# Sliding windows of a 2D image: loading the input in bands of 8 rows, issued between the stores

## The chip, the cores and the metric

One core of one Trainium2 chip runs the kernel. The metric is device time in microseconds (us) of one execution, as the median of several runs. The profile comes from one profiled execution; times in it count from the first instruction.

## The reference

The input `x` is float32 of shape (16, 64, 64, 64): image, channel, row, column. With a window of 8 and a stride of 4 there are 15 x 15 window positions, and each window is copied out:

```python
for i in range(n_h):
    for j in range(n_w):
        h_start = i * stride
        w_start = j * stride
        result[:, i, j] = x[:, :, h_start:h_start + window_size, w_start:w_start + window_size].copy()
```

Nothing is computed. 16.78 MB are read and 58.98 MB written, since each inner value stands in four windows.

## The kernel before, in words

The 128 partitions are 16 images x 8 channel groups; each partition holds 8 channels (`CLO`) of one image. The tile `L` has the whole input, 8 x 64 x 64 floats or 128 KB a partition, in one buffer that is written once.

Two DMAs fill it (lines 41 and 42), both issued on SP's queue: the upper 32 rows of every channel, then the lower 32. In memory 32 rows of a channel lie together, so a DMA consists of 128 x 8 runs of 8 KB.

Then 225 windows follow, row `i` outside and column `j` inside (lines 46 and 47). For each one VectorE copies the 8 x 8 x 8 floats of a window from `L` into a tile `g` (line 50), and a DMA stores `g` (line 51). In the output the 512 floats of a partition lie together, so a store is 128 runs of 2 KB, 256 KB in all. The pool of `g` has 28 buffers; a copy waits until the store of its buffer's last use has landed. Stores are issued in turn by SP (even windows) and ScalarE (odd ones): each of the two has a queue of its own, in the profile q1 (SP) and q10 (ScalarE; its sequencer is called ACTq).

What sets the order: each engine runs its own list of instructions in order, and the framework makes these lists when it builds the program, with a plan of its own of when each instruction could start. It follows the program text where an instruction can start by that plan, and takes a later one of the same engine first where it can't. So the order on a queue needn't be that of the text. In the built program SP's first store stands behind many of ScalarE's stores, and the last 20 stores of the list are all SP's.

The program has eight semaphores for these DMAs and gives them out in turn, in the planned order, over both queues. Before a DMA is issued, its queue waits until the DMA eight places earlier in that order has landed, whichever queue that was on. So at most eight are in flight. A copy waits for just those loads that wrote the part of `L` that it reads: the windows that lie in the upper 32 rows wait for the first load alone.

On the queue of an issuing engine everything waits behind the instruction at its head.

Of the kernel before, what the change touches and what calls it, by code (L numbers as in the profile page):

```python
# [1 line left out]

# [4 lines left out]


@with_exitstack  # L10
def kernel(
    ctx: ExitStack,
    tc: tile.TileContext,
    x: bass.AP,
    window_size: int,
    stride: int,
    out: bass.AP,
):
    nc = tc.nc
    P = nc.NUM_PARTITIONS  # L20

    B, C, H, W = x.shape
    Bo, NH, NW, Co, WSo, WSo2 = out.shape
    WS = int(window_size)
    ST = int(stride)
    assert Bo == B and Co == C and WSo == WS and WSo2 == WS

    f32 = mybir.dt.float32

    CHI = P // B  # L30
    CLO = C // CHI
    assert CHI * B == P and CLO * CHI == C

    lpool = ctx.enter_context(tc.tile_pool(name="lpool", bufs=1))
    gpool = ctx.enter_context(tc.tile_pool(name="gpool", bufs=28))

    L = lpool.tile([P, CLO, H, W], f32)

    HHALF = H // 2
    x_v = x.rearrange("b (ch cl) h w -> b ch cl h w", ch=CHI)  # L40
    nc.sync.dma_start(out=L[:, :, 0:HHALF, :], in_=x_v[:, :, :, 0:HHALF, :])
    nc.sync.dma_start(out=L[:, :, HHALF:H, :], in_=x_v[:, :, :, HHALF:H, :])

    trig = [nc.sync, nc.scalar]
    k = 0
    for i in range(NH):
        for j in range(NW):
            g = gpool.tile([P, CLO, WS, WS], f32, name="g")
            src = L[:, :, i * ST : i * ST + WS, j * ST : j * ST + WS]
            nc.vector.tensor_copy(out=g[:, :, :, :], in_=src)  # L50
            trig[k % 2].dma_start(out=out[:, i, j, :, :, :], in_=g[:, :, :, :])  # L51
            k += 1


# [1 line left out]
_INS = ['x', 'window_size', 'stride']  # L56
_OUTS = [((16, 15, 15, 64, 8, 8), 'float32')]
#: Inputs that are plain numbers.
_NUMBERS = {'window_size': 8, 'stride': 4}


# [26 lines left out]
```

## Time and profile before

| what | us |
|---|---|
| median of 3 runs | 221.94 (220.55, 221.94, 222.03) |
| span of the profiled execution, first to last instruction | 217.7 |
| VectorE busy | 88.7 |

The page of the profile gives the span of the profiled execution and no total of its own; the runs' median is 4.2 us above the span. A DMA packet in the profile is one run of bytes that one of the 16 DMA engines moves; the completion of a DMA is a small packet of its own on each engine. "Share" of a queue is the time of its packets over the time of 16 engines, so the shares of two queues can add to more than 100% where packets overlap.

### The profile page before, as it was taken

Reading aid. Unit: us, or ns where it says so; the run is one execution under the profiler, and the core shown is the slowest. Engines: PE = TensorE matmul, PEld = TensorE weight load, DVE = VectorE, ACT = ScalarE, POOL = GpSimd, SP = SyncE. Lnnn points to the kernel's source line nnn. Section 1 sums busy time; section 2 is a strip of 40 time slices with the busy share of each in tenths; the row PEclk is TensorE's granted clock in tenths of the full one; section 3 lists DMA queues with packets and bytes.
Section 4 is the critical chain, followed back from the end, with each engine's and each line's share of the span. In section 5 each row is a group of like instructions: output and inputs, shape, how many; then the busy total and the mean of one; then the engine's idle time right before and its main releaser. Section 6 shows DMA issues by size and latency. Waiting matters only on the chain.

```text
span 217.7 us, 824 instructions
## 1 busy us (share of the span) xinstructions
DVE 88.7 (41%) x225; POOL 0.2 (0%) x4
## 2 busy tenths in 40 slices
DVE  0000691124532446454565555555554554550000
POOL 0000000000000000000000000000000000000000
DMA  6999999989995999999999999999999999999997
GB/s 200 431 425 422 422 423 429 416 311 318 339 345 166 287 321 356 349 353 361 353 358 362 364 354 354 358 355 365 345 341 334 363 363 347 349 343 337 329 338 252
DMA packets 34487, 75.83 MB, mean 348 GB/s; under 512 B 3632, under 2 KB 3632, under 8 KB 32432
## 3 DMA queue, kind: packets, MB, share of 16 engines
q1 hardware_dynamic: 18352, 46.41, 59.0%
q10 hardware_dynamic: 16128, 29.37, 39.2%
q14 instruction: 7, 0.06, 0.1%
HBM read 16.78 MB, written 58.98 MB: 348 GB/s over the span
## 4 chain that ended last, share of the span: by engine, by line
DMA 82%; DVE 7%; issue 1%; DVEq 0%; ACTq 0%
DMA out_dram<-g 72%; DMA L<-in_x_dram 10%; DVE g L50 7%; DVEq L50 0%; ACTq L51 0%
## 5 line engine op out<-in xcount | busy, mean ns | idle before, releaser
L50 DVE COPY g<-L 128x512 f32<-128x512 f32 x225 | 88.7, 424 | 108.0 <-DMA out_dram<-g 83.4
L69 POOL MEMSET const-bfloat16-1.0<- 128x1 bf16 x1 | 0.1, 102 | 0.0
L69 POOL MEMSET const-uint8-127<- 128x1 uint8 x1 | 0.1, 102 | 0.0
L69 POOL MEMSET const-float32-1.0<- 128x1 f32 x1 | 0.1, 99 | 0.0
L69 POOL MEMSET const-float32-0.0<- 128x1 f32 x1 | 0.1, 98 | 0.2 <-issue 0.2
## 6 DMA issues: line engine op xcount, KB each, us to landing
out_dram<-g SPq DMA_DIRECT2D x113, 256.0 KB, 5.5
out_dram<-g ACTq DMA_DIRECT2D x112, 256.0 KB, 5.2
L<-in_x_dram SPq DMA_DIRECT2D x2, 8192.0 KB, 33.9
```

The source lines that it names most:

```text
L50: nc.vector.tensor_copy(out=g[:, :, :, :], in_=src)
L69: nc = _bacc.Bacc("TRN2", target_bir_lowering=False, num_devices=1)
```

## The change

The input is loaded in eight bands of 8 rows, each in four DMAs of two channels (512 KB, 256 runs of 2 KB), which go to SP and ScalarE in turn. The first band is issued ahead of everything. Every other band is issued in four pieces among the windows of the band before it: ahead of windows 0, 3, 6 and 9 of 15 for the first band, ahead of windows 0, 7, 14 and 21 of 30 for the later ones. The windows are taken in the same order as before; a band `n` brings window rows 2n - 1 and 2n. The pool of `g` has 36 buffers in place of 28.

```diff
@@ -29,33 +29,45 @@
 
     CHI = P // B
     CLO = C // CHI
-    assert CHI * B == P and CLO * CHI == C
+    RB = 8
+    NB = H // RB
+    assert CHI * B == P and RB == 2 * ST and WS == RB
 
     lpool = ctx.enter_context(tc.tile_pool(name="lpool", bufs=1))
-    gpool = ctx.enter_context(tc.tile_pool(name="gpool", bufs=28))
+    gpool = ctx.enter_context(tc.tile_pool(name="gpool", bufs=36))
 
     L = lpool.tile([P, CLO, H, W], f32)
+    x_v = x.rearrange("b (ch cl) (n r) w -> n (b ch) cl (r w)", ch=CHI, n=NB)
+    queues = [nc.sync, nc.scalar]
+    NP = 4
+    cw = CLO // NP
 
-    HHALF = H // 2
-    x_v = x.rearrange("b (ch cl) h w -> b ch cl h w", ch=CHI)
-    nc.sync.dma_start(out=L[:, :, 0:HHALF, :], in_=x_v[:, :, :, 0:HHALF, :])
-    nc.sync.dma_start(out=L[:, :, HHALF:H, :], in_=x_v[:, :, :, HHALF:H, :])
+    def load(n, k):
+        cs = slice(k * cw, (k + 1) * cw)
+        queues[k % 2].dma_start(out=L[:, cs, n * RB : (n + 1) * RB, :], in_=x_v[n, :, cs, :])
 
-    trig = [nc.sync, nc.scalar]
-    k = 0
-    for i in range(NH):
-        for j in range(NW):
+    for k in range(NP):
+        load(0, k)
+
+    t = 0
+    for n in range(NB):
+        rows = [i for i in (2 * n - 1, 2 * n) if 0 <= i < NH]
+        windows = [(i, j) for i in rows for j in range(NW)]
+        every = len(windows) // NP
+        for m, (i, j) in enumerate(windows):
+            if n + 1 < NB and m % every == 0 and m // every < NP:
+                load(n + 1, m // every)
             g = gpool.tile([P, CLO, WS, WS], f32, name="g")
             src = L[:, :, i * ST : i * ST + WS, j * ST : j * ST + WS]
             nc.vector.tensor_copy(out=g[:, :, :, :], in_=src)
-            trig[k % 2].dma_start(out=out[:, i, j, :, :, :], in_=g[:, :, :, :])
-            k += 1
+            queues[t % 2].dma_start(out=out[:, i, j, :, :, :], in_=g[:, :, :, :])
+            t += 1
 
 
 # ---- launch: one core; inputs and outputs as the reference has them ----
 _INS = ['x', 'window_size', 'stride']
 _OUTS = [((16, 15, 15, 64, 8, 8), 'float32')]
-#: Inputs that are plain numbers.
+
 _NUMBERS = {'window_size': 8, 'stride': 4}
 
 
```

## Rows read from the trace of the kernel before

**Rows 1.** The page: the span, 40 equal slices of 5.4 us, the chain of waits
```profile
span 217.7 us, 824 instructions
...
DMA  6999999989995999999999999999999999999997
GB/s 200 431 425 422 422 423 429 416 311 318 339 345 166 287 321 356 349 353 361 353 358 362 364 354 354 358 355 365 345 341 334 363 363 347 349 343 337 329 338 252
...
DMA 82%; DVE 7%; issue 1%; DVEq 0%; ACTq 0%
```

**Rows 2.** The page's groups: VectorE's copies; busy us, mean ns, idle us and releaser
```profile
L50 DVE COPY g<-L 128x512 f32<-128x512 f32 x225 | 88.7, 424 | 108.0 <-DMA out_dram<-g 83.4
```

**Rows 3.** Windows by stage: length, VectorE, GpSimd, TensorE clock, DMA share, GB/s
```profile
2.90:23.00 20.10, 0.00 (x0) 0.00 (x0) 1.00 1.00 418
26.00:44.00 18.00, 8.55 (x25) 0.00 (x0) 1.00 1.01 422
46.00:80.00 34.00, 13.98 (x36) 0.00 (x0) 1.00 0.88 287
80.00:196.00 116.00, 62.83 (x157) 0.00 (x0) 1.00 1.03 354
...
200.00:214.00 14.00, 0.00 (x0) 0.00 (x0) 1.00 0.99 331
```

**Rows 4.** DMA queues, 6 to 22 us: loads alone
```profile
DMA packets 831, 6.81 MB, mean 425 GB/s; under 512 B 0, under 2 KB 0, under 8 KB 0
```

**Rows 5.** DMA queues, 26 to 44 us: packets, MB, share of 16 engines
```profile
DMA packets 1448, 7.60 MB, mean 422 GB/s; under 512 B 64, under 2 KB 64, under 8 KB 672
...
q1 hardware_dynamic: 776, 6.36, 83.5%
q10 hardware_dynamic: 672, 1.25, 17.9%
```

**Rows 6.** DMA queues, 202 to 214 us: one queue of stores
```profile
DMA packets 2216, 4.04 MB, mean 337 GB/s; under 512 B 246, under 2 KB 246, under 8 KB 2215
...
q1 hardware_dynamic: 2215, 4.03, 99.6%
```

**Rows 7.** Timeline of the issuing queues: start us, us from first to last issue, count
```profile
24.25 4.57 ACTq L51 DMA_DIRECT2D out_dram<-g  x7
...
46.60 13.71 ACTq L51 DMA_DIRECT2D out_dram<-g  x17
...
58.63 1.48 SPq L51 DMA_DIRECT2D out_dram<-g  x2
```

**Rows 8.** Waits of SP's queue: us in total, times, longest us
```profile
SPq L51 <- DMA out_dram<-g: 80.1, 34, 56.4
```

**Rows 9.** DMA queues, 66 to 71 us: 40 slices of 0.125 us, tenths busy and GB/s
```profile
DMA  9998999510000000000000000004959789999979
GB/s 328 295 344 279 328 377 377 197 33 33 33 16 16 0 0 0 0 0 0 0 0 0 0 0 0 0 0 131 229 115 229 131 213 344 360 410 377 393 246 328
```

**Rows 10.** DMA queues, 82 to 194 us: stores from both queues
```profile
DMA packets 21735, 39.61 MB, mean 354 GB/s; under 512 B 2415, under 2 KB 2415, under 8 KB 21730
...
q1 hardware_dynamic: 10880, 19.82, 51.9%
q10 hardware_dynamic: 10850, 19.75, 51.1%
```

**Rows 11.** DMA queues, 0 to 4 us: 40 slices of 0.1 us, then packets
```profile
GB/s 0 0 0 0 0 0 0 0 0 0 0 0 0 0 0 0 0 0 0 0 0 164 410 573 164 0 0 0 246 0 0 164 164 492 492 164 328 655 328 246
DMA packets 56, 0.46 MB, mean 115 GB/s; under 512 B 0, under 2 KB 0, under 8 KB 0
```

**Rows 12.** The chain that ended last, its start: start us, us, what
```profile
0.73 22.70 DMA L<-in_x_dram
...
23.45 4.82 DVE g L50 x15
```

**Rows 13.** DMA queues, 212 us to the end: 40 slices of 0.14 us, GB/s
```profile
GB/s 417 388 302 359 316 417 359 302 345 331 417 359 359 374 359 417 316 230 345 316 374 345 331 359 316 446 388 359 216 58 14 0 0 0 0 0 0 0 0 0
```

## The prediction

> **What bounds the kernel now.** I read the page first: its span, the slices and the chain [rows 1]. The reader is to see that DMA holds 82% of the chain, that the DMA digits are nines nearly everywhere, and that the GB/s line beneath them still falls from about 425 to about 350 after slice 7. VectorE is busy 88.7 us of 217.7 and mostly waits for stores to free its buffers [rows 2]. So the bound is the 16 DMA engines, and the question is what they carry per us in each stage.
>
> The windows by stage come next [rows 3]: loads alone 418 GB/s (425 without the ramp, [rows 4]), loads beside a few stores 422 [rows 5], then 34 us at 287, then 116 us of stores from both queues at 354, then 14 us at 331. Two of these are worse than the 354 that this kernel keeps for most of its time:
> - 46 to 80 us: 34 x (1 - 287/354) = 6.4 us lost.
> - 200 to 214 us: 14 x (1 - 331/354) = 0.9 us lost. ScalarE's queue has nothing more; SP's works alone [rows 6].
>
> Why these two are so is in the queues [rows 7]: ScalarE issues seven stores from 24.25 us and then none until 46.60, when the second load has landed (seven stores and that load are the eight DMAs that may be in flight). SP's first store, the first of the program text, is issued only at 58.63, after a wait of 56.4 us [rows 8]; ScalarE has by then issued most of 24 (7 + 17). Until about 80 us the two queues are out of step and wait for each other's DMAs; around 67 to 69.5 us both are empty [rows 9]. At the end SP is some 20 stores behind.
>
> **What a 2 KB packet costs.** After the change every load run is 8 rows x 64 x 4 B = 2 KB instead of 8 KB. There is no 2 KB read in the trace of before, so I bound it.
> - From loads: beside stores, q1 took 83.5% of 16 engines x 18 us over 776 packets: 310 ns for 8 KB, a quarter is 77.5 ns. This is the lower end.
> - From stores beside loads: 17.9% x 288 us over 672 - 64 = 608 data packets (the 64 are the small completion packets) is 84.8 ns [rows 5].
> - From stores alone, two queues: (51.9 + 51.1)% x 1792 us over 21730 - 2415 = 19315 is 95.6 ns [rows 10]. One queue: 99.6% x 192 us over 2215 - 246 = 1969 is 97.1 ns [rows 6]. Upper end.
>
> The shares of [rows 10] add to 103%: neighbours overlap, so I divide 2 KB packets by 1.03. A store is 8 such packets on each engine, a load piece (128 partitions x 2 channels) 16. That gives
>
> store beside a load 8 x 84.8/1.03 = 0.66 us; store among stores 0.74 us (262144 B at 354 GB/s); load piece 16 x 84.8/1.03 = 1.32 us, between 1.20 (77.5 ns) and 1.49 (95.6 ns).
>
> I take 1.32: the same packet size on the same engines in a mixed stretch is the nearest row. A store is dearer among stores than beside a load, by 0.08 us, and the change puts loads beside more stores: that is its second effect.
>
> By the Trainium skill's "DMA: Bandwidth & Descriptors" (Bandwidth, "Where 436 GB/s comes from") the HBM side, about 358 GB/s, binds transfers between HBM and SBUF. The 354 of [rows 10] agrees for stores; the 425 of [rows 4] is against it for loads. It would make the whole traffic run at one rate, which is the second rival below.
>
> **The change part by part.**
> 1. *Loads.* Two DMAs of 8 MB go, 32 of 512 KB come: 32 x 1.32 = 42.2 us of engine time against 16.78 MB at 425 GB/s = 39.5 now. +2.7 us (bounds -1.1 to +8.2).
> 2. *No long head.* Now nothing is stored for 23.4 us, but the engines are full of loads then [rows 3], so this alone gives nothing; loads are only moved. Band 0 is 4 x 1.32 = 5.3 us from the effective start of data (0.46 MB by 4.0 us [rows 11], which is 1.1 us at 425, so 2.9), so it is in at 8.2. VectorE started about 0.6 us after the data now (8.39 MB at 425 from 2.9 ends at 22.6 to 22.9; its start is 23.45 [rows 12]). So copying starts near 8.8, the first store issues near 9.3, and its first packet follows 1.5 us later (issue 0.73 [rows 12], first bytes at 2.1 to 2.2 [rows 11]): 10.8. Meanwhile band 1's first piece is already on SP's queue (1.3 us), and the second on ScalarE's if the build lets it pass the unready stores: cover to 9.5 or 10.8. I charge 0.3 us (0 to 1.3).
> 3. *The disturbed stage goes.* Both queues now carry two pieces and 15 stores per band, in turn; neither has an 8 MB load in front of its stores, so I expect the built order to stay balanced: -6.4 us, and -0.9 for the one-queue end. If the order is uneven again, part of this stays.
> 4. *Stores beside loads.* While SP drains a piece, ScalarE's queue drains about as many bytes in stores, two per piece: 28 pieces x 2 = 56 stores at 0.66 instead of 0.74, -4.6 us; about seven stores already had that [rows 7], so -4.0 net. Bounds: 0, or all stores up to the last piece (39 come after it).
> 5. *Added waits.* VectorE's first copy of a band's second half waits for all four pieces of the next band, and every later copy queues behind it. The last piece is issued before window 21 of 30, so nine stores (six in the first band) and the following band's first piece lie behind it. Seven DMAs may be in flight behind it when it lands: 7 x 0.7 = 4.9 us. The turnaround is 0.6 (landing) + 0.42 (copy, [rows 2]) + 1.5 (to the first packet) = 2.5 us. Hidden, with 2.4 us to spare; what is late next is again the store's DMA. If the cover is gone, a boundary costs up to 2.5 us, seven times.
> 6. *Issues.* 16 more DMA issues on each queue. A store's issue takes 0.55 to 0.63 us when nothing blocks it (4.57 us for seven, [rows 7]); 16 x 0.65 = 10 us in 200, and where stores alone run the engines are busy all the time (103%), so the queues are ahead of them: 0. If they weren't, it is 10 us on each queue. Eight buffers more: VectorE is ahead anyway, 0.
>
> Sum as a whole: 2.9 start + 5.3 band 0 + 0.3 + 28 x 1.32 (37.0) + 56 x 0.66 (37.0) + 169 x 0.74 (125.1) + 1.6 end (last bytes near 216.1 [rows 13]) = 209.2 us. By differences: 217.7 + 2.7 + 0.3 - 6.4 - 0.9 - 4.0 = 209.4 us. They agree. The page gives a span of 217.7 and no total; the runs' median is 221.94, so 4.2 us lie around it. **Forecast 209.0 to 209.5 + 4.2 = 213.4 us.**
>
> **The rivals** (a measurement tells about 1% from no change: 219.7 to 224.2 is "same").
> - *The mix relieves the stores everywhere.* If what stretches store packets is the mean rate of writes, not the moment's, then all 186 stores up to the last piece cost 0.66: 130 more x 0.08 = 10.4 us less, about 203 us. For it: up to eight DMAs are in flight, so the 16 engines needn't be in the same DMA. Against: nowhere in the trace do stores make up most of a fast mix; 16% of the bytes is the most (1.25 of 7.60 MB, [rows 5]).
> - *One rate for all.* Reads and writes together run at the stores' 354: 75.8 MB / 354 = 214.1 + 2.9 + 0.3 + 1.6 = 218.9, 223.1 us: same as now. That is the rule cited above at work. For it: the 354 over 112 us. Against: 422 as soon as reads are in the mix [rows 5]. Between this and the forecast: load pieces at 1.32 but no gain for stores, 209.2 + 4.6 + 4.2 = 218 us.
> - *Band boundaries run dry (slower).* Where the built order or a slow landing puts the last piece of a band late, both queues run empty until VectorE has copied. The trace shows what it looks like: about 2 us of nothing from 67 us on [rows 9]. Seven boundaries at 2.5 are 17.5 us: 231 us. It decides from 8.5/7 = 1.2 us lost at each, that is when less than 1.3 us of DMA work lies behind the last piece at landing. Against it: 4.9 us by the count in step 5. In the Trainium skill's "DMA: Bandwidth & Descriptors" (Bandwidth, Measured) transfers under 1 MiB are advised against, with a fit of 2.0 us + bytes/436e3: an estimate from it is 3.2 us for a 512 KB piece, 102 us for 32 of them against 42 for the two of now, if nothing overlapped. The 256 KB stores at 354 GB/s [rows 10] show that overlap hides this here.
> - *The change isn't what it says.* The build orders each queue by its own plan; loads have nothing to wait for and could all be put first. Then the mix is gone and the sum is 218 us, as above.
>
> **How the numbers follow.** Forecast (own range 210 to 217) 0.48; relieved everywhere 0.18; no relief or loads first, 218 us, 0.12; one rate 0.11; boundaries dry 0.11. Faster by over 1%: 0.48 + 0.18 + 0.12 = 0.78; same 0.11; slower 0.11. The range 203 to 220 leaves out the dry boundaries, most of the one-rate case and the fastest tail.
>
> **What would show it.** Right: the first copy near 8.8 us; no stage below 340 GB/s after 11 us; stretches near 385 to 395 GB/s while a piece moves, near 354 otherwise, and over the bands a mean of about 365 to 370; the last 39 stores at 354 from both queues; VectorE waiting for loads at band starts without a hole in the DMA digits. Wrong: a mean near 395 (first rival), near 354 in mixed stretches (second), DMA digits below 9 every 26 us or so (third), or a long run of pure loads at the start (fourth).

## The result, and the profile after

Measured 212.69 us (four runs, 212.42 to 213.39) against 221.25 for the kernel before (four runs, 219.92 to 222.03); ratio 0.963, 95% interval 0.958 to 0.967. On record stood 213.4 us, range 203 to 220. The profiled execution took 212.9 us with a span of 211.1, so only 1.8 us lie around the span. In the experiments below, a run over 1.5% slower than the fastest of its kernel is left out of the median and of the ratio.

The page of the changed kernel answers to [rows 1] and [rows 2]:

```profile
span 211.1 us, 885 instructions
...
DMA  6999999999999999999999999999999999999997
GB/s 213 392 397 405 339 371 373 373 382 339 361 355 348 355 356 399 361 366 330 382 382 366 351 356 382 364 341 338 390 374 347 368 362 385 358 382 364 363 354 243
...
DMA 73%; DVE 14%; issue 4%; ACTq 0%; DVEq 0%; SPq 0%
...
L62 DVE COPY g<-L 128x512 f32<-128x512 f32 x225 | 76.2, 417 | 118.3 <-DMA L<-in_x_dram 101.0
```

The 5 in the DMA digits of [rows 1] and the 166 and 287 GB/s beneath it are gone; the 40 slices hold no hole. VectorE now waits for loads (101.0 us) where it waited for buffers, and that costs nothing while the digits stay at 9.

Rates by stage of the changed kernel (length, VectorE, GpSimd, TensorE clock, DMA share, GB/s), the counterpart of [rows 3]:

```profile
2.90:21.00 18.10, 11.93 (x36) 0.00 (x0) 1.00 1.05 397
21.00:37.00 16.00, 3.29 (x10) 0.00 (x0) 1.00 1.04 361
37.00:89.00 52.00, 20.39 (x60) 0.00 (x0) 1.00 1.03 362
89.00:141.00 52.00, 20.30 (x60) 0.00 (x0) 1.00 1.04 362
141.00:182.00 41.00, 10.15 (x30) 0.00 (x0) 1.00 1.03 364
182.00:194.00 12.00, 9.67 (x29) 0.00 (x0) 1.00 1.04 379
194.00:208.00 14.00, 0.47 (x2) 0.00 (x0) 1.00 1.03 356
```

The 34 us at 287 have no successor, and the last 14 us run at 356 on two queues instead of 331 on one. The bands run at 361 to 364 GB/s, near the 365 to 370 that the prediction named.

Inside a band the picture is the reverse of the forecast. The issues of three load pieces (start us, us, queue), and the rates around them:

```profile
109.88 0.38 ACTq L47 DMA_DIRECT2D L<-in_x_dram  x1
...
114.61 1.18 SPq L47 DMA_DIRECT2D L<-in_x_dram  x1
...
122.91 0.37 ACTq L47 DMA_DIRECT2D L<-in_x_dram  x1
```

```profile
111.40:113.40 2.00, 0.63 (x2) 0.00 (x0) 1.00 1.04 325
113.40:114.60 1.20, 0.00 (x0) 0.00 (x0) 1.00 1.02 379
114.60:117.00 2.40, 0.00 (x0) 0.00 (x0) 1.00 1.05 401
117.00:119.20 2.20, 0.00 (x0) 0.00 (x0) 1.00 1.03 303
119.20:122.90 3.70, 0.00 (x0) 0.00 (x0) 1.00 1.03 381
122.90:124.80 1.90, 0.00 (x0) 0.00 (x0) 1.00 1.06 388
124.80:127.00 2.20, 0.00 (x0) 0.00 (x0) 1.00 0.98 312
```

Some 1.5 to 2.5 us after each issue come about 2 us at 303 to 325 GB/s, with the engines still marked busy: the packets take longer (a 2 KB packet 113 ns from 117 to 119 us, against 86 from 114 to 117). By the completion packets in the trace, the piece issued at 114.61 moves from about 117.2 to 120.8 us and the one issued at 122.91 from about 124.5 to 128.0, so the slow stretch is the first part of a piece's own move. Between these stretches the rate is 379 to 401. The steady 354 of [rows 10] doesn't appear between the pieces here; at the end, when no load is left, the rate falls back to it (356).

### The profile page after: what moved, and what is told of

It is laid out like the page before. It is cut to its first block, busy times and chain, and to the rows that moved or that the text cites. A ratio compares the mean times of both kernels' runs of the same rounds, so it can differ in the third digit from the quotient of the medians.

```text
span 211.1 us, 885 instructions
## 1 busy us (share of the span) xinstructions
DVE 76.2 (36%) x225; POOL 0.2 (0%) x4
## 3 DMA queue, kind: packets, MB, share of 16 engines
q1 hardware_dynamic: 20624, 38.02, 51.3%
q10 hardware_dynamic: 20480, 37.76, 50.5%
HBM read 16.78 MB, written 58.98 MB: 359 GB/s over the span
## 4 chain that ended last, share of the span: by engine, by line
DMA 73%; DVE 14%; issue 4%; ACTq 0%; DVEq 0%; SPq 0%
DMA out_dram<-g 70%; DVE g L62 14%; DMA L<-in_x_dram 4%; ACTq L47 0%; DVEq L95 0%; ACTq L63 0%; DVEq L62 0%; SPq L63 0%
## 5 line engine op out<-in xcount | busy, mean ns | idle before, releaser
L62 DVE COPY g<-L 128x512 f32<-128x512 f32 x225 | 76.2, 417 | 118.3 <-DMA L<-in_x_dram 101.0
```

## The experiments

**All loads first, 2 KB runs as in the changed kernel.**

```diff
-    for k in range(NP):
-        load(0, k)
+    for n in range(NB):
+        for k in range(NP):
+            load(n, k)
...
-            if n + 1 < NB and m % every == 0 and m // every < NP:
-                load(n + 1, m // every)
```

> All 32 load pieces of 2 KB runs stand ahead of the stores, the window order and the 36 buffers stay. In the trace of the changed kernel each piece comes with some 2 us at 270 to 330 GB/s, and stores in between run at 390 to 400, falling to 355 within some 12 us after the last piece. Theory A (a load piece among the stores costs a slow stretch of its own, but the stores after it run faster for a while, and stores left alone fall back to 354): loads until about 46 us, then stores at 390 for some 10 us and at 354 after, 215 us in all, and a slow decay seen in the rates. Theory B (stores run at 390 wherever both queues are served in turn, so the pieces in between only harm): 202 us. Theory C, as forecast (stores 0.74 us among stores, 0.66 beside loads): 42 + 225 x 0.74 + 4.8 + 1.8 = 215 us with 354 GB/s from the first store on, and no decay.

215.39 us, ratio 0.968 (0.961 to 0.975). Its rates:

```profile
24.00:30.00 6.00, 0.00 (x0) 0.00 (x0) 1.00 1.05 387
...
48.00:54.00 6.00, 3.82 (x10) 0.00 (x0) 1.00 1.05 405
54.00:60.00 6.00, 3.75 (x10) 0.00 (x0) 1.00 1.06 402
60.00:66.00 6.00, 2.35 (x7) 0.00 (x0) 1.00 1.04 366
66.00:72.00 6.00, 3.24 (x9) 0.00 (x0) 1.00 1.03 354
```

A load piece at 387 GB/s is 524288 B / 387 = 1.35 us; the prediction took 1.32. Theory B falls: queues served in turn don't keep stores at 390. Stores alone start at 402 to 405 and fall to 354 within some 20 us. The total fits A and C alike, the decay fits A only.

**Big loads on both queues.** The kernel before, with its two loads cut by channels over SP and ScalarE:

```diff
-    nc.sync.dma_start(out=L[:, :, 0:HHALF, :], in_=x_v[:, :, :, 0:HHALF, :])
-    nc.sync.dma_start(out=L[:, :, HHALF:H, :], in_=x_v[:, :, :, HHALF:H, :])
+    for h in range(0, H, HHALF):
+        for q in range(2):
+            cs = slice(q * CLO // 2, (q + 1) * CLO // 2)
+            trig[q].dma_start(out=L[:, cs, h : h + HHALF, :], in_=x_v[:, :, cs, h : h + HHALF, :])
```

> The kernel before with each of its two 8 MB loads cut by channels into two of 4 MB, one on each queue, 8 KB runs as before; so neither queue is blocked alone and the planned order of the stores is even. Theory A and C: the stage of 46 to 80 us at 287 GB/s and the one-queue end are gone (7.3 us by the forecast), stores at 354: 221.3 - 7.3 = 214 us, or 212 with 2 KB packets not paid. Theory B: stores at 390 from the start, 199 us. Rival: the order isn't what cost those 7 us, and the time stays within 1% of 221.

212.56 us, ratio 0.953 (0.944 to 0.962): the whole gain, with no bands and no mixing. The rival (the order isn't the cost) falls, and B again. Stages and queues of this kernel are shown below, from its second set of runs.

**Bands of 16 rows.** `RB = 16`, `NP = 8`, window rows `range(4 * n - 1, 4 * n + 3)` for a band.

> Bands of 16 rows: 32 pieces of 512 KB as in the changed kernel, but one channel by 16 rows each, so runs of 4 KB; eight pieces among the windows of the band before. Theory A1 (the slow stretch beside each piece comes from the short runs of the loads): the stretches shrink to half or less, 28 x 0.3 = 8 us gained, 204 us. A2 (it comes from reading in among writes at all, whatever the run): same as the changed kernel, 212 us within 1%. Theory C: a load packet of 4 KB costs 9 ns less per 2 KB, 1 us gained, 211.5 us.

212.83 us, ratio 0.958 (0.952 to 0.965): as the changed kernel. A1 isn't borne out; the bands ran at 368 GB/s. Theory C has a wrong sum: 9 ns on 16 packets of each of 32 pieces are 4.6 us and not 1, and the run shows no such gain.

**Pieces of 256 KB.** `NP = 8` instead of 4.

> The changed kernel with eight pieces of one channel (256 KB) for each band instead of four of two: the same bytes and runs, twice as many pieces. If a slow stretch costs per piece (some 0.5 us net each), 28 more of them are 14 us: 226 us. If it costs per byte, or the reads only take their place, 212 us within 1%. If each piece renews the fast state of the stores after it, the stores spend more of the time in it and it gets faster, 208 us.

214.77 us, ratio 0.969 (0.961 to 0.976). The full price per piece (226) falls, and so does the gain (208). Whether 28 more pieces cost anything isn't shown: the interval overlaps that of the changed kernel (0.958 to 0.967), and from 37 to 182 us this kernel moves 362 GB/s, the rate of the changed kernel's bands.

**Second half in 1 MB pieces of 8 KB runs among the windows.**

```diff
+    for k in range(CLO):
+        load(0, k)
...
+            if t % 12 == 0 and t // 12 < CLO:
+                load(1, t // 12)
```

Here `load(n, k)` loads channel `k` of half `n` (32 rows).

> First half of the rows up front, second half in eight pieces of one channel by 32 rows (1 MB, 8 KB runs), each ahead of every twelfth of the first 96 windows. In the changed kernel pieces of 2 KB runs among stores slow everything to 270 to 330 GB/s for 2 us, bands of 16 rows (4 KB runs) are about as fast in total. A1 (short runs cause it): no slow stretch beside the pieces, 400 GB/s or more until the last piece at window 84, then 400 for some 12 us and 354 after: 2.9 + 20 + 33.4 MB at 405 (82) + 34 MB at 360 (94) + 1.6 + 1.8 = 203 us. A2 (reads among writes cost whatever the run): slow stretches stay, 211 to 213 us.

215.77 us, ratio 0.975 (0.966 to 0.984). A1 falls. In the built order two of the eight pieces follow the first half at once, and six come among the stores. Rates near three of these, and after the first two of the three:

```profile
40.00:48.00 8.00, 3.68 (x10) 0.00 (x0) 1.00 0.98 310
48.00:52.00 4.00, 0.85 (x2) 0.00 (x0) 1.00 1.03 394
68.00:72.00 4.00, 1.62 (x4) 0.00 (x0) 1.00 0.98 286
72.00:76.00 4.00, 0.43 (x1) 0.00 (x0) 1.00 0.99 386
92.00:96.00 4.00, 0.00 (x0) 0.00 (x0) 1.00 1.03 296
```

The slow stretches are there with 8 KB runs too. So it isn't the run length: a piece that comes among stores slows the traffic for a while, one of 1 MB for about 4 us. The last of the six, issued at 96.92 us, is an exception: from 100 to 108 us the rate is 402. A2's 211 to 213 us was a little too good.

**The second half of the bands as one block.** Bands 0 to 3 up front, bands 4 to 7 (16 pieces) together ahead of window 60.

> As with all loads first, but bands 4 to 7 (16 pieces, 2 KB runs) follow as one block ahead of window 60. The fast start of the stores is over within some 14 us in that run. If reading (or not writing) for some 20 us renews it, the rates show 400 GB/s twice, once after each block of loads, each falling to 350 within 14 us: 215.4 - 1.8 = 213.5 us. If it comes only from the first stores of a run (their place in memory, or full buffers), the second stage starts at 350 and the time is 215.4 within 1 us.

213.95 us, ratio 0.970 (0.965 to 0.975).

```profile
24.00:42.00 18.00, 9.73 (x25) 0.00 (x0) 1.00 1.05 405
42.00:56.00 14.00, 7.49 (x20) 0.00 (x0) 1.00 1.04 367
69.00:88.00 19.00, 0.00 (x0) 0.00 (x0) 1.00 1.05 390
88.00:92.00 4.00, 0.76 (x2) 0.00 (x0) 1.00 1.03 385
92.00:100.00 8.00, 4.57 (x12) 0.00 (x0) 1.00 1.04 362
100.00:200.00 100.00, 43.92 (x115) 0.00 (x0) 1.00 1.03 350
```

The first stores run at 405 for 18 us. After the second block 385 lasts some 4 us at most, then 362 and 350: the high rate is renewed weakly, and neither alternative of the expectation describes it. The total is as the first one said.

**A pause.** All loads first; ahead of window 120 the queues are drained and VectorE copies into a spare tile.

```diff
+            if t == 120:
+                tc.strict_bb_all_engine_barrier()
+                for _ in range(24):
+                    nc.vector.tensor_copy(out=pad[:, :, :, :], in_=L[:, :, 0:WS, 0:WS])
+                tc.strict_bb_all_engine_barrier()
```

> All loads first, and ahead of window 120 all queues are drained and nothing is moved while VectorE makes 24 copies (10 us), then the stores go on. Nothing of the output is left out. If time without writes renews the fast state, the rates after the pause start near 400 GB/s and fall to 350 within some 14 us; if only reads renew it, they start at 350. Total some 215 + 14 = 229 us either way.

229.48 us, one run.

```profile
48.00:60.00 12.00, 7.62 (x20) 0.00 (x0) 1.00 1.05 405
66.00:132.00 66.00, 21.66 (x57) 0.00 (x0) 1.00 1.03 350
133.00:145.00 12.00, 10.37 (x25) 0.00 (x0) 1.00 0.01 2
146.00:148.00 2.00, 2.00 (x7) 0.00 (x0) 1.00 0.72 202
148.00:160.00 12.00, 12.00 (x37) 0.00 (x0) 1.00 1.03 350
```

12 us without traffic renew nothing: after the start-up at 202 the stores run at 350 at once.

**28 buffers.** The changed kernel with `bufs=28`.

> The changed kernel with 28 buffers of g as before. The prediction charged nothing for the eight more: 212.7 us within 1%. If the deeper pool is what lets VectorE stop for the loads without a gap, it is slower, 215 us or more.

212.92 us, ratio 0.964 (0.958 to 0.970): the eight buffers are worth nothing that can be measured.

**The main three once more, and the queues made uneven**, on one chip. The last one differs from the changed kernel in one place:

```diff
-        queues[k % 2].dma_start(out=L[:, cs, n * RB : (n + 1) * RB, :], in_=x_v[n, :, cs, :])
+        nc.sync.dma_start(out=L[:, cs, n * RB : (n + 1) * RB, :], in_=x_v[n, :, cs, :])
```

> The changed kernel itself, beside the next three on one chip. 212 to 213.5 us, ratio to the kernel before 0.955 to 0.967.

> All pieces of 2 KB runs ahead of the stores, once more. If putting loads among the stores gains something (forecast 4.0 us, first runs 2.7), it is 2 to 4 us above the changed kernel on the same chip; if it gains nothing, within 1 us.

> Four 4 MB loads of 8 KB runs on two queues, once more. By packets alone 2.7 us below the loads first in 2 KB runs, so within 1 us of the changed kernel: the changed kernel's gain over the kernel before is then the even order of the queues, and its two other effects cancel.

> The changed kernel with all pieces on SP's queue. The bytes, runs and places of the loads stay; SP now carries 8.4 MB more than ScalarE, and the planned order gets bunches of SP's stores. If turn-taking of the queues is what the gain rests on, some of the 7 us comes back, 215 to 219 us. If only the long block of one queue behind 8 MB loads was to blame, 212.7 within 1%.

| kernel | us | ratio to before (220.67 us) | 95% interval |
|---|---|---|---|
| changed kernel | 211.49 | 0.959 | 0.954 to 0.964 |
| all loads first, 2 KB runs | 214.86 | 0.974 | 0.970 to 0.978 |
| big loads on both queues, 8 KB runs | 212.50 | 0.962 | 0.957 to 0.968 |
| changed kernel, all loads on SP | 223.67 | 1.013 | 1.008 to 1.018 |

The first two intervals don't meet: loads among the stores gain 3.4 us. Big loads and the changed kernel can't be told apart. In the run with big loads both queues issue their stores from 24 us on (start us, us from first to last issue, count), the loads run no faster than before (423 GB/s, 422 to 425 in [rows 4] and [rows 5]), and no stage is below 350:

```profile
24.13 181.44 SPq L53 DMA_DIRECT2D out_dram<-g  x113
...
24.47 180.81 ACTq L53 DMA_DIRECT2D out_dram<-g  x112
...
2.90:42.00 39.10, 9.48 (x28) 0.00 (x0) 1.00 1.01 423
42.00:54.00 12.00, 5.60 (x15) 0.00 (x0) 1.00 1.04 394
54.00:66.00 12.00, 6.39 (x18) 0.00 (x0) 1.00 1.04 361
66.00:200.00 134.00, 63.23 (x166) 0.00 (x0) 1.00 1.03 350
```

With all loads on SP the whole gain is lost, and more than I gave even the theory for it (215 to 219). Three stages of that run, then the bands of the changed kernel on the same chip:

```profile
9.00:18.00 9.00, 5.12 (x15) 0.00 (x0) 1.00 0.87 268
18.00:36.00 18.00, 10.15 (x30) 0.00 (x0) 1.00 1.02 351
36.00:186.00 150.00, 50.83 (x150) 0.00 (x0) 1.00 1.02 350
...
37.00:182.00 145.00, 51.16 (x151) 0.00 (x0) 1.00 1.04 369
```

Two places pay most. At the start ScalarE's queue has no piece to bridge the wait for VectorE: 9 us at 268 where the changed kernel had 397, 9 x (1 - 268/397) = 2.9 us. In the bands the rate is 350 and not 369: 150 x (1 - 350/369) = 7.7 us. Together that is 10.6 of the 13.3 us between the two spans (222.2 and 208.9). Queue shares over the span with all loads on SP:

```profile
q1 hardware_dynamic: 24976, 46.41, 60.8%
q10 hardware_dynamic: 16128, 29.37, 38.9%
```

In the changed kernel the two are at 51.3% and 50.5%. Why the uneven queues are slower with the engines as busy was not tried further. The split of a moment isn't it: from 105 to 118 us it is 68 to 35, and the rate 363. The traces say only where the time is lost: the six lowest slices of 3 us in the bands are at 253 to 285 GB/s with all loads on SP and at 305 to 313 in the changed kernel's first profile, while the highest reach 400 in both.

None of these versions beats the changed kernel beyond the uncertainty; big loads on both queues equal it with less code.

## Why the prediction was right, and where it wasn't

The span was forecast as 209.2 and measured as 211.1; what lies around it as 4.2 us and measured as 1.8. Both errors have one origin: the profiled execution of the kernel before was a short one. Single executions of that kernel differ by 2 to 3 us; one with a span of 217.7 took 219.5 us, 2.4 less than the median of 221.94 from which the 4.2 came. So the trace's rates were a little too good, and what was missing was booked as time around the span. In the total the two errors cancel, since 217.7 + 4.2 is the median: from it the forecast takes 8.5 us (221.94 - 213.4), and 8.6 were measured (221.25 - 212.69). That the total fits says little of the single terms. For the three large ones the runs on one chip give +2.4, -8.2 and -3.4 us, each known to some 1 to 1.5 us by the intervals in the table.

1. *Loads in 2 KB runs, +2.7 us.* Right in size: 214.86 - 212.50 = 2.4 us between loads first in 2 KB runs and big loads on both queues; 1.35 us for a piece against 1.32. By the rate of the loads alone it is more: 16.78 MB at 387 GB/s are 43.4 us, 3.9 more than 39.5. The first stores give some of it back, which the prediction didn't have: behind big loads they run at 394 GB/s for 12 us, behind 2 KB loads at 404 for 15 (the second run with all loads first):

```profile
45.00:60.00 15.00, 7.62 (x20) 0.00 (x0) 1.00 1.05 404
```

2. *Start.* Right in its times, too cautious in its charge. The chain and the first issues of the changed kernel:

```profile
1.28 7.59 DMA L<-in_x_dram
...
9.07 3.11 DVE g L62 x9
```

```profile
0.73 2.36 ACTq L47 DMA_DIRECT2D L<-in_x_dram  x4
```

The first copy is at 9.07 (8.8 forecast). The built order let all four pieces of band 1 pass the unready stores, two on each queue (I had counted on one or two), so nothing was bare until 21 us at 397 GB/s. The run with all loads on SP shows what a bare start costs.

3. *The disturbed stage, -7.3 us.* Right, and the main thing: big loads on both queues, with runs, bytes and windows as before, gain 8.2 us (220.67 - 212.50). The fast first stores are part of that: 12 us at 394 and 12 at 361 instead of 350 are worth 1.9 us, where the forecast had 354 throughout. Uneven queues lose everything again, though not in the same way, as the engines stay busy in that run's bands. The Trainium skill's "DMA: Bandwidth & Descriptors" (Issuing engines are not separate DMA queues) says that issuing from several engines only saves the time of issuing. The runs disagree for this kernel: all 32 loads on SP instead of 16 on each queue cost 12.2 us (223.67 - 211.49), while the issue of a piece takes some 0.45 to 0.49 us, and SP isn't short of time to issue: its stores wait 53.3 us in all for other stores to land.
4. *Stores beside loads, -4.0 us.* The size came out (3.4 us), but by luck: the place was wrong. I had it that stores are cheap while a piece moves (385 to 395 GB/s) and cost 0.74 us otherwise (354). The trace shows 303 to 325 for about 2 us of each piece and 379 to 401 in between. The step that failed is the price "store beside a load", taken from 16% of stores beside an 8 MB load [rows 5] and carried over to pieces that come among stores; and the price "store among stores", taken from a stretch that had been without loads for 35 us [rows 10]. Both were off, in opposite directions, and the mean of a band (361 to 364 against 365 to 370) hardly noticed.
5. *Added waits, 0.* Right: six waits of VectorE for loads, 101.0 us in all, the longest 22.2, and a DMA share of 1.03 to 1.04 in all stages of the bands. The boundaries never ran dry. The waits fall on the first copy of a band, for that band's own pieces; step 5 of the prediction has them at a band's second half, which changes nothing in its sum.
6. *Issues and buffers, 0.* Right: a piece's issue has a median of 0.45 us on SP and 0.49 on ScalarE, and 28 buffers do as well. (SP gets 14 more issues and not 16, since two loads were its own before.)

Of the rivals, "relieved everywhere" was half right in kind (stores between pieces do run at 390) and missed the slow stretches that pay for it. "One rate for all" was wrong in kind, since the mix swings between 303 and 401, though its 354 lies near the mean of 362. "Loads first" is the run at 214.86, 3 us under the 218 I gave it: 1.3 of them because the kernel before took 220.67 on that chip and not 221.94, and besides its first stores run at 404. The fit that the third rival quotes from the Trainium skill's "DMA: Bandwidth & Descriptors" stands there under "Anatomy of one DMA — SWDGE (gpsimd) path", for a DMA issued from GpSimd; the pieces here are issued by SP and ScalarE, and in a row they take 1.35 us each and not 3.2.

## What to carry to other kernels

Before cutting transfers finer, look at which queue a big transfer blocks and what the other queue does meanwhile: here four lines that give each queue half of the loads bring as much as bands and pieces together. A rate read from a long steady stretch is a price for that stretch; the same stores ran at 350, 390 and 405 GB/s by what had gone before, so a mixed stage wants a mixed row or both ends. And take the time around the span from an execution that has both numbers.

## What was not expected of the hardware

- Stores alone start at 394 to 405 GB/s after the initial loads, for 12 to 18 us in these runs, and settle at 350 to 352. A pause of 12 us doesn't bring that rate back, a block of pure loads does so for some 4 us at most, single pieces among the stores bring 379 to 401 between them.
- A load piece among stores is accompanied by some 2 us (512 KB) or 4 us and more (1 MB) at 286 to 325 GB/s, for runs of 2 KB and of 8 KB alike, while all 16 engines count as busy. One 1 MB piece of six had no such stretch.

What makes either is open. That the first stores write to a certain place in the output was not tried apart, but the place alone isn't it: between pieces stores run at 379 to 401 in the middle of the output too. The engines' position relative to each other and the memory's own state can't be told apart by these runs.
